# Input projection of a hybrid attention block: queries, SGU values and compressed keys/values with tokens stationary and weights moving

## The chip, the cores and the metric

The kernel runs on one core of a Trainium2 chip: TensorE (PE) with its weight loads (PEld), VectorE (DVE), ScalarE (ACT), GpSimd (POOL) and the DMA queues, one on SyncE (SP) and one on GpSimd. The metric is the device time of one execution in microseconds.

## The reference

One layer over 256 latent tokens with 256 context tokens as a prefix; everything is fp32, the model is 2048 wide. What matters here is the first half:

```python
h = _modulate(_rms(x, norm1_g), sh1, sc1)             # ctx_h likewise, from the context
proj = h @ w_in     # columns: q 512 | kv 256 + rotary key 64 | u 1024 | v 1024 | gates 4096
q = _rms(proj[:, :512], q_norm_g) @ w_uq              # 8 heads of 128 + 64, rotary, normed
kv = _rms(kv_in[:, :256], kv_norm_g) @ w_ukv          # kv_in: those columns of h and of ctx_h
k = _rms(concat([k_nope, k_rope]), qk_norm_k)
attn_o = attention(q, k, v)                           # over 512 keys
vn = layernorm(gelu(v_in)) * norm_g + norm_b
sgu_o = gelu(u_in) * (w_s @ vn + b_s)                 # in chunks of 128 tokens, 8 groups
merged = (sigmoid(ga) * (attn_o @ w_br_attn) + sigmoid(gb) * (sgu_o @ w_br_sgu)) @ w_out
```

After it stand a gated residual, a second norm and a SwiGLU feed-forward with 5632 hidden columns.

## The kernel before

**Precision.** A matrix product is made of three fp32r matmuls: both operands are split into a high part (`hi`, ACT copies to fp32r, line 230) and the difference (`lo`, DVE, line 231), and `mm3` adds hi x hi, hi x lo and lo x hi. Activations live in tiles `g` ("slots" of 128 x 512, 60 of them), with hi in columns 0 to 255 and lo in 256 to 511. `mm(out, lhsT, rhs)` (line 244) keeps `lhsT` in the array and streams `rhs`; in the profile `mm<-g,whi` is activations moving past standing weights, `mm<-whi,g` the other way round.

**Weights.** Class `W` loads them in pieces of 1024 columns (512 KB) into 10 buffers `raw` by SP's queue and splits each into parts of 512 columns in 8 buffers `whi` and 8 `wlo`.

**Input projection.** The string `ORDER` names the order of items: `M` (modulation vectors for some k-tiles of the hidden state, which end in the normed and split k-tiles `hs`, and `hc` for the context), `X` (loads the context), `C` (a chunk of the projection), `K` (a chunk of compressed keys/values), `A` (the norms of the latents). The 16 k-tiles come in six groups (`KGROUPS`: 2, 2, 2, 2, 4, 4), since they become ready one after the other; in each group all 24 column tiles of 128 are computed (`NT_IN`: 4 of Q, 8 of V, 8 of U, 4 of the gates) and added to the sums `acc` in SBUF, by ACT for the first group and by DVE (line 554) after. `in_chunk` and `kv_chunk` keep a weight tile of 128 x 128 standing and move 256 tokens, so the results have columns on partitions. `kv_chunk` has three column tiles, the third with the 64 rotary columns twice, for latents and context. PSUM has 4 banks `mm` for products and 4 `aux` for the rest. A scheduler orders the instructions of each engine; each engine then works in its order.

**Norms of the latents.** `latents` squares the sums, adds the squares over partitions and channels with fp32 matmuls against a matrix `ones`, makes 1/sqrt of whole rows of 256 or 512 columns (`rms_rstd`, `rsqrt`, lines 285 to 300), scales and splits.

**Gating (SGU).** V is needed with tokens on partitions for the layer norm, so PE transposes 16 tiles (line 650), ACT copies them out of PSUM (line 653), and DVE takes statistics. While this goes on, PE computes gate columns: `fill` hands out pieces of the rest of the gates (`fill_items`), and with each of them background pieces of the second modulation (`wmod2`), which DVE adds into `acc` (line 416) and whose results go through DRAM (`m_d`, lines 439 to 446, on POOL's queue).

**Attention.** Heads go in pairs. The factors `rk` of the key norms are written to DRAM (`rk_d`, line 757) and broadcast to 128 partitions, one DMA a head (line 782, POOL's queue), at the start of each pair; the first step of DVE on the scores (line 794) multiplies by them. ACT takes exp (line 800), DVE scales (line 802), PE transposes (line 805). `fill` again puts gate columns in between.

Of the kernel before, what the change touches and what calls it, by code (L numbers as in the profile page):

```python
# [13 lines left out]
P = 128  # L14
# [98 lines left out]
def block_kernel(  # L113
# [100 lines left out]
    class W:  # L214


        def __init__(self, src, ncols, split=True):
            self.raw = []
            self.parts = []
            for s in range(0, ncols, WHALF):  # L220
                n = min(WHALF, ncols - s)
                raw = wp.tile([P, WHALF], F32, tag="raw", name=f"raw{uid()}", bufs=RAW_BUFS)
                nc.sync.dma_start(raw[:, :n], src[P * s:P * (s + n)].rearrange("(p f) -> p f", p=P))
                self.raw.append(raw)
                if split:
                    for q in range(0, n, WPART):
                        e = min(WPART, n - q)
                        hi = wp.tile([P, WPART], F32R, tag="whi", name=f"whi{uid()}")
                        lo = wp.tile([P, WPART], F32R, tag="wlo", name=f"wlo{uid()}")
                        S.activation(hi[:, :e], raw[:, q:q + e], AF.Copy)  # L230
                        V.tensor_tensor(out=lo[:, :e], in0=raw[:, q:q + e], in1=hi[:, :e].bitcast(F32),  # L231
                                        op=ALU.subtract)
                        self.parts.append((hi, lo))

        def cols(self, c0, n=P):
            hi, lo = self.parts[c0 // WPART]
            c0 %= WPART
            return hi[:, c0:c0 + n], lo[:, c0:c0 + n]
# [239 lines left out]

    def latents(acc_q, acc_kv):
# [7 lines left out]
        rq0 = slot()  # L487
        rms_rstd(rq0[:, 0:256], ps[:, 0:256], Q_LORA, 256)
        for k in range(4):
            v = slot()[:, 0:256]  # L490
            V.scalar_tensor_tensor(out=v, in0=acc_q[k // 2][:, (k % 2) * 256:(k % 2 + 1) * 256],
                                   scalar=pcol(PR_QN + k), in1=rq0[:, 0:256], op0=ALU.mult, op1=ALU.mult)
            t = slot(F32R)
            split_to(t[:, 0:256], t[:, 256:512], v)
            qn.append(t)


        ps = auxbank()
        for k in range(2):
            sq = slot()  # L500
            S.activation(sq, acc_kv[k], AF.Square)
            mm(ps, ones, sq, k == 0, k == 1)
        rk0 = slot()
        rms_rstd(rk0, ps, KV_LORA, 512)
        for k in range(2):
            v = slot()
            V.scalar_tensor_tensor(out=v, in0=acc_kv[k], scalar=pcol(PR_KVN + k), in1=rk0,
                                   op0=ALU.mult, op1=ALU.mult)
            hi, lo = slot(F32R), slot(F32R)
            split_to(hi, lo, v)  # L510
# [10 lines left out]
    acc = [slot() for _ in range(NT_IN // 2)]  # L521
# [15 lines left out]
    def in_chunk(g, ts):  # L537
        ks = KGROUPS[g]
        nk = len(ks)
        n = len(ts) * nk * P  # L540
        w = W(flat(win, off[0], n), n)
        off[0] += P * n
        for ti, t in enumerate(ts):
# [4 lines left out]
            for ki, k in enumerate(ks):  # L548
                mm3(ps[:, h * 256:(h + 1) * 256], w.cols((ti * nk + ki) * P), hilo(hs[k]),
                    ki == 0, ki == nk - 1)  # L550
            if h == 1 and g == 0:
                S.activation(acc[i], ps, AF.Copy)
            elif h == 1:
                V.tensor_tensor(out=acc[i], in0=ps, in1=acc[i], op=ALU.add)  # L554

    acc_kv = [slot() for _ in range(NT_KV)]
    koff = [0]

    def kv_chunk(ks):
        nk = len(ks)  # L560
        w = W(flat(wkv, koff[0], NT_KV * nk * P), NT_KV * nk * P)
        koff[0] += P * NT_KV * nk * P
        for t in range(NT_KV):
            ps = mmbank()
            for src, o in ((hs, 0), (hc, 256)):
                for ki, k in enumerate(ks):
                    mm3(ps[:, o:o + 256], w.cols((t * nk + ki) * P), hilo(src[k]), ki == 0, ki == nk - 1)
            if ks[0] == 0:
# [8 lines left out]
            "A": [lambda: latents(acc[0:2], acc_kv)]}  # L577
# [59 lines left out]
    for i in range(4):  # L637
        S.activation(acc_v[i], acc_v[i], AF.Gelu)
# [119 lines left out]

    fill(UQ_GATES[4], GATE_RATE)
# [16 lines left out]
    for p in range(HEADS // 2):  # L776
        pair = (2 * p, 2 * p + 1)
        rkb, pts = {}, {}
        for h in pair:
            rkb[h] = slot()  # L780
            r = 2 * (h % 4) + h // 4
            nc.gpsimd.dma_start(rkb[h], rk_d[r:r + 1, :].to_broadcast([P, 512]))
# [228 lines left out]
def _layout(inp):  # L1011
# [44 lines left out]
    for ang in (row, col):  # L1056
# [79 lines left out]
```

## Time and profile before

| | |
|---|---|
| median of 3 runs | 1457.03 us (1454.49 to 1457.6) |
| profiled execution | 1455.91 us, its span 1454.1 us |
| PE busy | 1422.4 us (98% of the span), 8782 matmul records |
| DVE, ACT busy | 1018.6 us (70%), 772.6 us (53%) |
| DMA | 356.08 MB, mean 245 GB/s |
| granted TensorE clock, mean | 0.995 |

The span is the time from the first to the last instruction; the rest of the execution lies around it. "Busy" on PE counts the modelled length of matmuls, which overlap, so what one matmul costs is read from the distance between starts. The columns of a timeline are: start in us, length in us, engine, line, operation, out<-in, shape, count of merged instructions, and in brackets the idle time before and what ended it.

### The profile page before, as it was taken

Reading aid. Unit: us, or ns where it says so; the run is one execution under the profiler, and the core shown is the slowest. Engines: PE = TensorE matmul, PEld = TensorE weight load, DVE = VectorE, ACT = ScalarE, POOL = GpSimd, SP = SyncE. Lnnn points to the kernel's source line nnn. Section 1 sums busy time; section 2 is a strip of 40 time slices with the busy share of each in tenths; the row PEclk is TensorE's granted clock in tenths of the full one; section 3 lists DMA queues with packets and bytes.
Section 4 is the critical chain, followed back from the end, with each engine's and each line's share of the span. In section 5 each row is a group of like instructions: output and inputs, shape, how many; then the busy total and the mean of one; then the engine's idle time right before and its main releaser. Section 6 shows DMA issues by size and latency. Waiting matters only on the chain.

```text
span 1454.1 us, 23911 instructions
## 1 busy us (share of the span) xinstructions
PE 1422.4 (98%) x8782; PEld 1215.1 (84%) x8782; DVE 1018.6 (70%) x1738; ACT 772.6 (53%) x1432; POOL 22.2 (2%) x44
## 2 busy tenths in 40 slices
PE   6999999999989999999999999999999999999998
PEld 4898899886767799988788888888888888888887
DVE  2676579896688688999866666666666667786553
ACT  4655457555534554555566555555555554444442
POOL 0000000000101000000000000000000000000000
PEclk9999999999999999999999999999999999999999
DMA  9987874785499498999553555555555568898560
GB/s 366 350 318 266 316 297 140 253 287 190 144 313 314 175 362 329 324 353 391 175 183 135 192 188 186 192 188 189 187 190 189 188 202 308 309 361 302 198 213 33
DMA packets 104167, 356.08 MB, mean 245 GB/s; under 512 B 12520, under 2 KB 14824, under 8 KB 104048
## 3 DMA queue, kind: packets, MB, share of 16 engines
q1 hardware_dynamic: 102096, 350.82, 67.0%
q0 software_dynamic: 1952, 3.72, 1.0%
q8 instruction: 69, 1.13, 0.3%
q14 instruction: 50, 0.41, 0.1%
HBM read 352.36 MB, written 2.13 MB: 244 GB/s over the span
## 4 chain that ended last, share of the span: by engine, by line
PE 65%; DVE 4%; DMA 1%; issue 1%; ACT 0%; DVEq 0%; ACTq 0%
PE mm L244 62%; PE ax L244 2%; DVE acc L416 1%; DMA raw<-in_wmod_dram 1%; DVE wlo L231 1%; PE ax L805 0%; DVE g L802 0%; ACT g L800 0%; DVE g L405 0%; DVE g L890 0%; DVE g L794 0%; DVE g L870 0%; DVE g L892 0%; ACT whi L230 0%; DVE g L402 0%
## 5 line engine op out<-in xcount | busy, mean ns | idle before, releaser
L244 PE MATMUL mm<-g,whi 128*128 128x512 f32 (+1 forms) x3456 | 878.6, 347 | 0.8 <-ACT g L702 0.5
L230 ACT ACTIVATE whi<-raw 128x512 fp32r<-128x512 f32 x897 | 557.3, 630 | 500.9 <-PE mm L244 349.9
L231 DVE TENSOR_TENSOR wlo<-raw,whi 128x512 fp32r<-128x512 f32 x897 | 604.1, 687 | 259.1 <-ACT whi L230 253.4
L244 PE MATMUL mm<-g,wlo 128*128 128x256 f32 x2656 | 588.7, 282 | 0.6 <-DVE wlo L231 0.6
L244 PEld LDWEIGHTS mm<-g,wlo 128*128 128x128 f32 x2656 | 495.3, 190 | 79.5 <-DVE wlo L231 1.3
L244 PEld LDWEIGHTS mm<-g,whi 128*128 128x128 f32 x3456 | 540.0, 191 | 22.1 <-issue 11.0
L244 PE MATMUL mm<-whi,g 128*128 128x512 f32 x992 | 308.3, 391 | 0.0
L244 PEld LDWEIGHTS mm<-whi,g 128*128 128x128 f32 x992 | 186.2, 188 | 41.3 <-issue 2.5
L244 PE MATMUL mm<-wlo,g 128*128 128x512 f32 x496 | 193.2, 390 | 0.2 <-DVE wlo L231 0.2
L416 DVE SCALAR_TENSOR_TENSOR acc<-raw,silw,acc 128x1024 f32<-128x1024 f32 x120 | 153.4, 1278 | 17.7 <-DMA raw<-in_wmod_dram 17.1
L244 PEld LDWEIGHTS mm<-wlo,g 128*128 128x128 f32 x496 | 93.1, 188 | 21.2 <-issue 1.1
L554 DVE TENSOR_TENSOR g<-mm,g 128x512 f32<-128x512 f32 x60 | 41.1, 686 | 26.4 <-PE mm L244 25.9
L279 ACT ACTIVATE g<-g 128x256 fp32r<-128x256 f32 (+1 forms) x106 | 41.9, 414 | 13.7 <-DVE g L973 8.2
L280 DVE TENSOR_TENSOR g<-g,g 128x256 fp32r<-128x256 f32 (+1 forms) x106 | 43.2, 424 | 7.4 <-ACT g L279 7.3
L971 DVE TENSOR_TENSOR g<-mm,g 128x256 f32<-128x256 f32 x88 | 33.3, 419 | 17.3 <-ACT g L970 17.2
L970 ACT ACTIVATE g<-mm 128x256 f32<-128x256 f32 x88 | 29.0, 381 | 30.9 <-PE mm L244 30.9
L244 PE MATMUL ax<-g,g 128*128 128x128 f32 (+2 forms) x224 | 42.6, 374 | 0.0
L244 PE MATMUL ax<-raw,silw 128*32 128x256 f32 (+1 forms) x576 | 33.4, 359 | 3.7 <-DMA raw<-in_wmod_dram 3.7
L244 PEld LDWEIGHTS ax<-g,g 128*128 128x128 f32 (+1 forms) x224 | 26.6, 190 | 11.5 <-issue 9.6
L244 PEld LDWEIGHTS ax<-raw,silw 128*32 128x32 f32 x576 | 16.9, 109 | 16.0 <-DMA raw<-in_wmod_dram 5.8
L800 ACT ACTIVATE g<-g,nb,rq 128x512 f32<-128x512 f32 x16 | 13.0, 812 | 17.5 <-DVE nb L798 17.4
L375 ACT ACTIVATE g<-g,m 128x256 f32<-128x256 f32 x32 | 17.6, 592 | 8.3 <-DVE m L364 5.3
(140 smaller groups left out, 471.1 us busy)
## 6 DMA issues: line engine op xcount, KB each, us to landing
raw<-in_wmod_dram SPq DMA_DIRECT2D x192, 512.0 KB, 6.3
raw<-in_wffi_dram SPq DMA_DIRECT2D x176, 512.0 KB, 3.2
raw<-in_wffo_dram SPq DMA_DIRECT2D x88, 512.0 KB, 4.9
raw<-in_wgate_dram SPq DMA_DIRECT2D x56, 512.0 KB, 4.7
raw<-in_win_dram SPq DMA_DIRECT2D x48, 512.0 KB, 7.7
raw<-in_wout_dram SPq DMA_DIRECT2D x32, 512.0 KB, 7.5
raw<-in_wbrs_dram SPq DMA_DIRECT2D x16, 512.0 KB, 9.2
raw<-in_wbra_dram SPq DMA_DIRECT2D x16, 512.0 KB, 6.5
```

What stands on the lines that cost most here:

```text
L230: S.activation(hi[:, :e], raw[:, q:q + e], AF.Copy)
L231: V.tensor_tensor(out=lo[:, :e], in0=raw[:, q:q + e], in1=hi[:, :e].bitcast(F32), op=ALU.subtract)
L244: nc.tensor.matmul(out, lhsT, rhs, start=start, stop=stop)
L279: S.activation(dst_hi, src, AF.Copy)
L280: V.tensor_tensor(out=dst_lo, in0=src, in1=dst_hi.bitcast(F32), op=ALU.subtract)
L375: S.activation(v, v, AF.Identity, bias=m[:, 2 * jj + s:2 * jj + s + 1], scale=m[:, 2 * n + 2 * jj + s:2 * n + 1 + 2 * jj + s])
L416: V.scalar_tensor_tensor(out=acc, in0=w.raw[0], scalar=sil[:, k, 0:1], in1=acc, op0=ALU.mult, op1=ALU.add)
L554: V.tensor_tensor(out=acc[i], in0=ps, in1=acc[i], op=ALU.add)
L800: exp = S.activation(t, t, AF.Exp, bias=nb, scale=rq[:, col:col + 1], accum_out=sm)
L970: S.activation(d, ps[:, 256:512], AF.Copy)
L971: V.tensor_tensor(out=d, in0=ps[:, 0:256], in1=d, op=ALU.add)
```

## The change

Q, V and the compressed keys/values are computed the other way round: 128 tokens stand (`rows_of`: the hi or lo half of a k-tile of `hs`), and 512 (Q: one block, V: two, called `T`) or 320 weight columns move. The results have tokens on partitions: a `T` block fills two banks, one for each half of the tokens; kv makes four tiles of 128 tokens x 320. U and the gates stay (`F`). Weight pieces of kv are 960 columns, its parts 320. The latents' norms are taken by rows (`unit_rows`: an ACT square with its sum, small operations on 128 x 2 or 128 x 4, a DVE scaling), and PE then transposes the normed rows (8 tiles for Q, 12 for kv), after which `scaled_parts` applies the gain and splits. V needs no transposes in the gating stage. The broadcasts of `rk` are issued one head pair ahead (`key_rows`), odd pairs into `rst` and a part of `cst` that are no longer read.

```diff
+    items = [("T", b) for b in range(NB_T)] + [("F", t) for t in range(NT_F)]
...
+    def unit_rows(tiles, n):
+
+        ssq = small(len(tiles), f"ssq{n}", 1)
+        for i, t in enumerate(tiles):
+            S.activation(slot()[:, 0:n], t[:, 0:n], AF.Square, accum_out=ssq[:, i:i + 1])
+        r = small(len(tiles), f"rr{n}", 1)
+        rms_rstd(r, ssq, n, len(tiles))
+        for i, t in enumerate(tiles):
+            V.tensor_scalar_mul(t[:, 0:n], t[:, 0:n], r[:, i:i + 1])
...
+        unit_rows(acc_q, Q_LORA)
         for i in range(2):
-            sq = slot()
-            S.activation(sq, acc_q[i], AF.Square)
-            for k in range(2):
-                mm(ps[:, 0:256], ones, sq[:, k * 256:(k + 1) * 256], i + k == 0, i + k == 2)
...
+            ps = auxbank()
+            for j in range(2):
+                for tt in range(2):
+                    k = 2 * i + j
+                    nc.tensor.transpose(ps[:, j * 256 + tt * P:j * 256 + (tt + 1) * P],
+                                        acc_q[tt][:, k * P:(k + 1) * P], ident)
...
+            if kind == "T":
+                ps = [mmbank(), mmbank()]
+                for ki, k in enumerate(ks):
+                    for tt in range(2):
+                        mm3(ps[tt], rows_of(hs, k, tt), w.cols(c0 + ki * 512, 512), ki == 0, ki == nk - 1)
+                for tt in range(2):
+                    summed(g, acc_t[t][tt], ps[tt])
...
-        for t in range(NT_KV):
-            ps = mmbank()
-            for src, o in ((hs, 0), (hc, 256)):
-                for ki, k in enumerate(ks):
-                    mm3(ps[:, o:o + 256], w.cols((t * nk + ki) * P), hilo(src[k]), ki == 0, ki == nk - 1)
...
+        for t, src in enumerate((hs, hs, hc, hc)):
+            ps = mmbank()[:, 0:KV_COLS]
+            for ki, k in enumerate(ks):
+                mm3(ps, rows_of(src, k, t % 2), w.cols(ki * KV_COLS, KV_COLS), ki == 0, ki == nk - 1)
+            summed(ks[0], acc_kv[t][:, 0:KV_COLS], ps)
...
-            ps = auxbank()
-            for i in range(4):
-                j = half * 4 + i
-                nc.tensor.transpose(ps[:, i * P:(i + 1) * P],
-                                    acc_v[j // 2][:, (j % 2) * 256 + n * P:(j % 2) * 256 + (n + 1) * P], ident)
-            d = slot()
-            S.activation(d, ps, AF.Copy)
-            V.bn_stats(out=st[:, half * 6:(half + 1) * 6], in_=d)
-            nat.append(d)
+            V.bn_stats(out=st[:, half * 6:(half + 1) * 6], in_=nat[half])
...
+        for h in (2 * p, 2 * p + 1):
+            rkb[h] = slot() if p % 2 == 0 else (rst, cst[:, 2 * P:2 * P + TOK])[h % 2]
...
+        if p + 1 < HEADS // 2:
+            key_rows(p + 1)
```

On PE, the first chunk of the projection before the change; the product banks are `mm`, the first name behind the arrow moves, the second stands (`g_230` and `g_287` are the first two k-tiles):

```order
L244 MATMUL mm_310<-g_230,whi_292 128x256 x2
L244 MATMUL mm_310<-g_230,wlo_293 128x256
L244 MATMUL mm_324<-g_230,whi_296 128x256 x2
L244 MATMUL mm_310<-g_287,whi_292 128x256
L244 MATMUL mm_324<-g_230,wlo_297 128x256
L244 MATMUL mm_324<-g_287,whi_296 128x256
```

The same place after it (`g_231` and `g_288` are the k-tiles now; line 244 has become 255):

```order
L255 MATMUL mm_311<-whi_293,g_231 128x512
L255 MATMUL mm_312<-whi_293,g_231 128x512
L255 MATMUL mm_311<-wlo_294,g_231 128x512
L255 MATMUL mm_311<-whi_293,g_231 128x512
L255 MATMUL mm_312<-wlo_294,g_231 128x512
L255 MATMUL mm_312<-whi_293,g_231 128x512
L255 MATMUL mm_311<-whi_297,g_288 128x512
```

Weights and tokens have changed sides, a matmul is 512 columns wide, and two banks are filled together.

On PE at the norm of Q's latents before the change, in the last third of the chunk after Q's last one (`ax_2798` is the bank of the sums):

```order
L244 MATMUL mm_2772<-g_2403,whi_2742 128x256 x2
L244 MATMUL mm_2772<-g_2403,wlo_2743 128x256
L244 MATMUL ax_2798<-g_2799,ones 128x256 x2
L244 MATMUL ax_2798<-g_2803,ones 128x256 x2
L244 MATMUL mm_2896<-g_2102,whi_2878 128x256 x2
L244 MATMUL mm_2896<-g_2102,wlo_2879 128x256
```

After it, between the first V block (`mm_2429`, `mm_2430`; called T1 below, Q's block is T0) and the second (`mm_2576`, T2); `g_161` and `g_162` are the normed rows of Q:

```order
L255 MATMUL mm_2430<-wlo_2426,g_2128 128x512
L255 MATMUL mm_2430<-whi_2425,g_2128 128x512
L512 MATMUL ax_2474<-cst,g_161 128x128
L512 MATMUL ax_2474<-cst,g_162 128x128
L512 MATMUL ax_2474<-cst,g_161 128x128
L512 MATMUL ax_2474<-cst,g_162 128x128
L512 MATMUL ax_2485<-cst,g_161 128x128
L512 MATMUL ax_2485<-cst,g_162 128x128
L512 MATMUL ax_2485<-cst,g_161 128x128
L512 MATMUL ax_2485<-cst,g_162 128x128
L255 MATMUL mm_2576<-whi_2558,g_1875 128x512
```

On DVE, what makes those rows ready stands like this after the change (line 561 adds T0's two banks, 242 is the split of weights, 310 to 305 the small operations, 498 the scaling):

```order
L561 TENSOR_TENSOR g_161<-mm_2381,g_161 128x512
L561 TENSOR_TENSOR g_162<-mm_2382,g_162 128x512
L242 TENSOR_TENSOR wlo_2573<-raw_2566,whi_2572 128x512
L310 TENSOR_SCALAR g_2463<-ssq_2457 128x2
L242 TENSOR_TENSOR wlo_2607<-raw_2604,whi_2606 128x512
L302 RECIPROCAL g_2465<-g_2465 128x2
L303 TENSOR_TENSOR g_2466<-g_2463,g_2465 128x2
L242 TENSOR_TENSOR wlo_2611<-raw_2604,whi_2610 128x512
L304 SCALAR_TENSOR_TENSOR g_2466<-g_2466,g_2465 128x2
L305 SCALAR_TENSOR_TENSOR rr_2462<-g_2466,g_2465 128x2
L498 TENSOR_SCALAR g_161<-g_161,rr_2462 128x512
L498 TENSOR_SCALAR g_162<-g_162,rr_2462 128x512
```

The transposes depend on the end of this chain, where the `ones` matmuls depended on the squares alone. The 12 transposes of kv stand 24 + 33 matmuls further on.

On POOL, the DMA issues around the head pairs before the change:

```order
L757 DMA rk_d<-g_4439 2x512 x4
L782 DMA g_4546<-rk_d 128x512
L782 DMA g_4548<-rk_d 128x512
L439 DMA m_d_4823<-g_4821 16x1x16 x4
L442 DMA sh_158<-m_d_4823 128x8x1
L782 DMA g_4922<-rk_d 128x512
L782 DMA g_4924<-rk_d 128x512
```

And after it:

```order
L783 DMA rk_d<-g_4067 2x512 x4
L793 DMA g_4082<-rk_d 128x512
L793 DMA g_4084<-rk_d 128x512
L793 DMA rst<-rk_d 128x512
L793 DMA cst<-rk_d 128x512
L450 DMA m_d_4453<-g_4451 16x1x16 x4
L453 DMA sh_158<-m_d_4453 128x8x1
L793 DMA g_4552<-rk_d 128x512
L793 DMA g_4554<-rk_d 128x512
```

The second pair's broadcasts (`rst`, `cst`) stand ahead of the `m_d` transfers now, right behind the first pair's.

## Rows read from the trace of the kernel before

**Rows 1.** Busy time on the page: us, share of the span, instructions.

```profile
PE 1422.4 (98%) x8782; PEld 1215.1 (84%) x8782; DVE 1018.6 (70%) x1738; ACT 772.6 (53%) x1432; POOL 22.2 (2%) x44
```

**Rows 2.** Stretches: length, busy us by engine, granted PE clock, DMA share, GB/s.

```profile
24.00:212.00 188.00, 184.82 (x1719) 166.50 (x1720) 124.25 (x238) 97.15 (x192) 0.00 (x0) 0.98 0.83 320
212.00:300.00 88.00, 87.97 (x600) 80.76 (x599) 77.45 (x143) 57.57 (x99) 0.00 (x0) 1.00 0.61 210
...
397.00:480.00 83.00, 76.27 (x420) 59.37 (x420) 72.48 (x120) 35.56 (x70) 9.43 (x16) 0.96 0.90 309
```

**Rows 3.** Timeline of PE in the input projection; eight triples lie between the two.

```profile
70.81 0.28 PE L244 MATMUL mm<-g,wlo 128*128 128x256 f32 x1
...
73.69 0.28 PE L244 MATMUL mm<-g,wlo 128*128 128x256 f32 x1
```

**Rows 4.** Timeline of PE in the last projection; eight triples lie between the two.

```profile
1222.14 0.39 PE L244 MATMUL mm<-wlo,g 128*128 128x512 f32 x1
...
1227.58 0.39 PE L244 MATMUL mm<-wlo,g 128*128 128x512 f32 x1
```

**Rows 5.** Timeline of PE at Q's norm and at the gating stage's transposes.

```profile
216.60 0.28 PE L244 MATMUL mm<-g,wlo 128*128 128x256 f32 x1
216.72 1.89 PE L244 MATMUL ax<-g,ones 128*128 128x256 f32 x8
...
218.68 0.28 PE L244 MATMUL mm<-g,wlo 128*128 128x256 f32 x1
...
266.00 1.91 PE L650 MATMUL ax<-cst,g 128*128 128x128 f32 x16
```

**Rows 6.** Timeline at the second norm, whose chain is the nearest to the new one.

```profile
705.98 0.63 ACT L893 ACTIVATE g<-g 128x512 f32<-128x512 f32 x1 [3.06 <-DVE g L892]
706.52 0.19 ACT L893 ACTIVATION_READ_ACCUMULATOR g<-g 128x1 f32 x1
...
708.19 0.38 PE L244 MATMUL ax<-dg,g 128*128 128x128 f32 x1 [1.65 <-DVE dg L908]
```

**Rows 7.** Groups by line and shape: busy us, mean ns, idle us before, its releasers.

```profile
L231 DVE TENSOR_TENSOR wlo<-raw,whi 128x512 fp32r<-128x512 f32 x895 | 603.5, 688 | 259.1 <-ACT whi L230 253.4 <-DMA raw<-in_wffi_dram 2.8 <-DMA raw<-in_wmod_dram 0.3
...
L230 ACT ACTIVATE whi<-raw 128x512 fp32r<-128x512 f32 x895 | 556.7, 630 | 500.9 <-PE mm L244 349.9 <-DVE wlo L231 70.1 <-DMA raw<-in_win_dram 26.8
...
L554 DVE TENSOR_TENSOR g<-mm,g 128x512 f32<-128x512 f32 x60 | 41.1, 686 | 26.4 <-PE mm L244 25.9
...
L802 DVE TENSOR_SCALAR g<-g,sm 128x512 f32<-128x512 f32 x16 | 7.7, 483 | 0.3
...
L290 ACT ACT_TABLE_LOAD x4 | 5.1, 1283 | 0.1
```

**Rows 8.** Timelines of POOL, DVE and PE at the second head pair.

```profile
404.53 1.09 POOL L782 DMA_DIRECT2D g<-rk_d  x2
...
412.52 0.69 DVE L794 CUSTOM_DVE_ANT_0 g<-ax,g 128x512 f32<-128x512 f32 x1 [3.29 <-DMA g<-rk_d]
...
412.91 0.40 PE L244 MATMUL mm<-g,whi 128*128 128x512 f32 x1
416.97 0.45 PE L805 MATMUL ax<-cst,g 128*128 128x128 f32 x1 [3.66 <-DVE g L802]
```

**Rows 9.** Two stretches behind that gap, columns as in rows 2.

```profile
416.90:422.50 5.60, 5.53 (x19) 4.89 (x20) 5.02 (x9) 2.12 (x5) 0.00 (x0) 0.50 0.83 251
422.60:428.00 5.40, 5.40 (x31) 4.43 (x31) 4.70 (x7) 2.71 (x5) 0.00 (x0) 1.00 0.97 351
```

**Rows 10.** The third pair: issue, landing of these broadcasts, DVE's step, PE's wait.

```profile
446.76 0.56 POOL L782 DMA_DIRECT2D g<-rk_d  x1
...
DMA to landing us min/median/max: 6.5/7.5/8.6
...
453.44 0.69 DVE L794 CUSTOM_DVE_ANT_0 g<-ax,g 128x512 f32<-128x512 f32 x1 [2.37 <-PE mm L244]
...
458.41 0.63 PE L805 MATMUL ax<-cst,g 128*128 128x128 f32 x4 [2.49 <-DVE g L802]
```

More of the change, by code (lines that the diff above doesn't have):

```diff
@@ L99, in in_chunks @@
 def in_chunks():
+    items = [("T", b) for b in range(NB_T)] + [("F", t) for t in range(NT_F)]
     out = []
     for g, ks in enumerate(KGROUPS):
-        c = max(1, (WCOLS // P) // len(ks))
-        out += [(g, list(range(i, min(i + c, NT_IN)))) for i in range(0, NT_IN, c)]
+        room = 0
+        for it in items:
+            if room == 0:
+                out.append((g, []))
+                room = WCOLS // P // len(ks)
+            out[-1][1].append(it)
+            room -= 4 if it[0] == "T" else 1
     return out
@@ new lines, in latents @@
+            for j in range(2):
+                t = slot(F32R)
+                scaled_parts(t[:, 0:256], t[:, 256:512], ps[:, j * 256:(j + 1) * 256], pcol(PR_QN + 2 * i + j))
+                qn.append(t)
+        unit_rows(acc_kv, KV_LORA)
+        for t in acc_kv:
+            V.tensor_copy(t[:, KV_COLS:KV_COLS + ROPE], t[:, KV_LORA:KV_COLS])
+        turned_kv = []
+        for k in range(3):
+            ps = auxbank()
+            for tt in range(4):
+                nc.tensor.transpose(ps[:, tt * P:(tt + 1) * P], acc_kv[tt][:, k * P:(k + 1) * P], ident)
+            turned_kv.append(ps)
@@ L518, in latents @@
         V.tensor_copy(krot[:, 256:512], kg[:, 256:512])
-    acc = [slot() for _ in range(NT_IN // 2)]
+    acc_t = [[slot() for _ in range(2)] for _ in range(NB_T)]
+    acc = [slot() for _ in range(NT_F // 2)]
     chunks = in_chunks()
@@ L535, in block_kernel, with summed, rows_of, in_chunk @@
     pcur = {}
-    def in_chunk(g, ts):
+    def summed(g, d, ps):
+        if g == 0:
+            S.activation(d, ps, AF.Copy)
+        else:
+            V.tensor_tensor(out=d, in0=ps, in1=d, op=ALU.add)
+    def rows_of(src, k, tt):
+        return src[k][:, tt * P:(tt + 1) * P], src[k][:, 256 + tt * P:256 + (tt + 1) * P]
+    def in_chunk(g, items):
         ks = KGROUPS[g]
         nk = len(ks)
-        n = len(ts) * nk * P
+        n = sum(4 if kind == "T" else 1 for kind, _ in items) * nk * P
         w = W(flat(win, off[0], n), n)
         off[0] += P * n
-        for ti, t in enumerate(ts):
+        c0 = 0
+        for kind, t in items:
+            if kind == "T":
[5 more added lines that the diff above has]
+                    summed(g, acc_t[t][tt], ps[tt])
+                c0 += nk * 512
+                continue
             i, h = divmod(t, 2)
@@ L548, in in_chunk @@
             for ki, k in enumerate(ks):
[L549 to L556, printed above, removed]
+                mm3(ps[:, h * 256:(h + 1) * 256], w.cols(c0 + ki * P), hilo(hs[k]), ki == 0, ki == nk - 1)
+            if h == 1:
+                summed(g, acc[i], ps)
+            c0 += nk * P
+    acc_kv = [slot() for _ in range(4)]
     koff = [0]
@@ L576, in block_kernel @@
             "K": [lambda ks=ks: kv_chunk(ks) for ks in kv_groups()],
-            "A": [lambda: latents(acc[0:2], acc_kv)]}
+            "A": [lambda: latents(acc_t[0], acc_kv)]}
     for o in ORDER:
         todo[o].pop(0)()
-    acc_v = [acc[2 + i] for i in range(4)]
-    acc_u = [acc[6 + i] for i in range(4)]
-    gate_a, gate_b = acc[(NT_IN - NT_GE) // 2:], []
+    acc_v = acc_t[NB_Q:]
+    acc_u = acc[0:NT_U // 2]
+    gate_a, gate_b = acc[NT_U // 2:], []
     sgo = []
@@ L636, in block_kernel @@
     sg = [row_bcast(RW_SG + i) for i in range(4)]
-    for i in range(4):
-        S.activation(acc_v[i], acc_v[i], AF.Gelu)
+    for v in acc_v:
+        for t in v:
+            S.activation(t, t, AF.Gelu)
     for i in range(4):
@@ L777, in block_kernel @@
         pair = (2 * p, 2 * p + 1)
[L778 to L782, printed above, removed]
+        pts = {}
+        if p + 1 < HEADS // 2:
+            key_rows(p + 1)
         for qt in range(2):
```

84 lines of the change are left out of this document (36 added, 48 removed).

## Prediction

> **What bounds the kernel now.** I read the totals first. TensorE (PE) is busy 1422.4 of 1454.1 us [rows 1], so the question is where it waits and where it is only kept full. The table by stretches answers that: in the input projection (24 to 212 us) it is busy 184.8 of 188 us, while the DMA engines are busy 83% of the time; in the gating stretch (212 to 300) it is busy 87.97 of 88; in the attention (397 to 480) it is busy 76.3 of 83, with VectorE (DVE) at 72.5 and the DMA engines at 90%, and the granted clock averages 0.96 [rows 2]. So up to 300 us work taken from PE is time, as long as ScalarE (ACT) and DVE deliver; in the attention waits count.
>
> **Price of a matmul.** In the input projection eight triples of 256 columns, from 70.81 to 73.69 us, take 2.88 us, which is 120 ns a matmul [rows 3]. In the last projection, where weights move and tokens stand, eight triples of 512 columns take 5.44 us, 226.7 ns each [rows 4]. At 2.4 GHz (the granted clock averages 0.98 over the first stretch [rows 2]) 256 columns alone are 106.7 ns and 512 are 213.3, so both rows leave 13.3 ns for each matmul with its own weight load. Fewer, wider matmuls save 13.3 ns each.
>
> **Token blocks (T).** Twelve column tiles, Q's 4 and V's 8, were 12 x 16 x 3 = 576 matmuls of 256 columns; they become 3 x 16 x 2 x 3 = 288 of 512, the same columns. 576 x 120 - 288 x 226.7 ns = 69.1 - 65.3: **-3.8 us**.
>
> The page "TensorE: Matmul & The Clock Gate" of the Trainium skill, section "Back-to-back issue gap", gives an isolated matmul its columns at 2.4 GHz plus about 2.5 ns. By that this term would be -0.7 us, and the kv term below -5.4. The trace disagrees, with 13.3 ns at both widths.
>
> **Compressed keys/values (kv).** Before: 3 tiles, the third the rotary columns twice, x 2 sources x 16 x 3 = 288 matmuls of 256. After: 4 token tiles x 16 x 3 = 192 of 320, the rotary columns once. No row has 320 columns. The bounds are the two rows, 120 and 226.7 ns: 192 of them take 23.0 to 43.5 us against 34.6 before, so from -11.5 to +9.0. I take the straight line between them, 146.7 ns, because both rows lie on it with the same 13.3 ns: 28.2 us, **-6.4 us**.
>
> **Norms of the latents.** Removed on PE: the matmuls against `ones`. Between the matmul at 216.60 and that at 218.68 us 0.36 us would pass without them; 2.08 did, so Q's four cost 1.7 us [rows 5]; kv's two have twice the columns each, so I estimate as much again. Added: 8 and 12 transposes. Sixteen such ran in the gating stage in 1.91 us, end of the last included [rows 5]; started one behind the other that is some 0.11 us each, 2.2 us for 20. Together **-1.2 us**. The 16 of the gating stage, where PE has no gap [rows 2], go: **-1.8 us**; the four ACT copies behind them cost nothing, since PE had work of the gates over them.
>
> **The wait that this adds.** Before, PE needed only squares for its `ones` matmuls, and the long row arithmetic ran beside other matmuls. Now PE's transposes need the whole chain: add, square, root, scale. The nearest chain of its kind (line 893 to the transposing matmuls of the second norm) takes 2.21 us from the square's start, with PE waiting the last 1.65 of them [rows 6]. Q's stands in the order behind one block, T1, of 24 matmuls: 5.4 us of cover. From the end of T0 I count the second add 0.69, one weight copy 0.63, two squares of about 0.8 with their accumulators, a weight copy 0.63, then the small operations, about 1.4 (706.71 to 708.19 in rows 6), two weight differences of 0.69 among them, and two scalings of 0.48 [rows 6, 7]: 6.4 us with what overlaps. So PE waits some 1.0 us. Behind the transposes stands T2, and everything after it. The kv transposes have T2 and 33 matmuls of 256 as cover, 9.4 us, and ahead of them in ACT's queue lie Q's four scaled copies, a Gelu, some four weight copies, four squares and two table loads of 1.28 [rows 7], about 10 us, and then DVE's chain of about 3: 2 us late. **+3 us**; bounds 0 (the scheduler placed them to fit) and 7 (both chains twice as late).
>
> **Banks and weight parts.** A block holds two PSUM banks and fills them together, so the third block waits for both adds of the first; a kv group holds all its weight parts until its fourth token tile, where before they came free one by one. Each add is 0.69 us, and DVE had time over before them: of 60 adds the queue stood idle before many, 25.9 us in all, waiting for PE [rows 7]. The DMA engines at 83% have room too; if PE needs 10 us less of 188 the share is about 88%. I take **+1.5 us**, bounds 0 and 5.
>
> **Key rows (rk) ahead.** Before, the second head pair's two broadcasts were issued at 404.53 us, and the score step of DVE (line 794) sat idle 3.29 us until 412.52 for the first of them; PE had run out at 413.3 and stood until 416.97, 3.66 us [rows 8]. Behind that gap the clock is at half: 19 matmuls in 5.6 us, and 31 in the 5.4 us after it at full clock [rows 9], so 2.3 us more are lost. The third pair's step began at 453.44, after 2.37 us of idleness that the view puts on PE; these broadcasts land 6.5 to 8.6 us after issue, and were issued from 446.76 on, so I read it as the broadcast again; PE then waited 2.49 us [rows 10]. Now each pair's broadcasts stand in GpSimd's queue one pair (some 35 us) earlier, ahead of the `m_d` stores, which wait for ACT anyway. PE's upper bound is 3.66 + 2.3 + 2.49 = 8.5 us. But DVE has only 10.5 us of idleness in those 83 us, 5.7 of it this wait, and the DMA engines 8 [rows 2, 8, 10]: what is late next is DVE's own queue and the weights. I take **-5 us**, bounds 0 and -8.5.
>
> **Sum.** -3.8 - 6.4 - 1.2 - 1.8 + 3 + 1.5 - 5 = -13.7. The profiled execution took 1455.9 us (span 1454.1 and 1.8 around it), so 1442.2; it lies 1.1 under the median of the runs, so by the median 1457.0 - 13.7 = **1443 us**.
>
> **Rivals.**
> - *The broadcasts are hidden, but another wait takes their place*: PE's gaps at 413 and 456 stay, with half a clock behind the first. For it: DVE and DMA are nearly full there. Against: DVE stood idle in both gaps. 1448 us.
> - *The chains of the norms eat the gain*: both waits and the banks at their upper bounds, +12 instead of +4.5: 1451 us. For it: ACT's queue in order. Against: before, PE waited nowhere in that stretch.
> - *320 columns cost what 512 do*: +9.0 instead of -6.4, 1458 us, no change. Only the missing row speaks for it.
> - *Slower: a stop of PE at the transposes long enough to drop the clock*, as after the 3.66 us gap. It decides when the two stops add up to more than 15 us (instead of 3), each with 2.3 us at half clock behind it; two stops of 9 us give 1463. Against it: the whole Q chain counted above is 6.4 us and has 5.4 of cover.
> - *The 13.3 ns belong to the columns, not to the matmul*: then T gives nothing, and kv gives its columns alone, 61,440 for 73,728, a sixth of 34.6, 5.8 us. Against it: the two rows have the same rest at 256 and at 512 columns [rows 3, 4]. 1448 us. The Trainium skill's section cited above comes near this case with its 2.5 ns a matmul; the trace speaks against both.
>
> **How the numbers follow.** Forecast (1437 to 1447, its own range) 0.62; other wait in the attention 0.13; chains 0.10; columns 0.04; slower 0.03; smaller gap 0.03; below 1437, all hidden and the attention giving 8.5, 0.05. From 1436 to 1450 I hold 0.8. A change within 0.2% (2.9 us) can't be told from none: faster 0.91 (all but the chains' far end, columns and slower), same 0.05, slower 0.04.
>
> **What would show it.** Right: in the input projection 512-column matmuls with weights moving 227 ns apart and the 320 ones 147; the gating stretch starts some 7 us earlier; a wait of about 1 us before the Q transposes and 2 before kv's; no idle DVE before the second pair's scores; no half clock in the attention. Wrong: gaps of more than 3 us at the transposes, gaps before the third block of a group, or the attention as long as before.

## The result and the profile after

The changed kernel takes **1431.7 us** (median of 4 runs, 1430.63 to 1432.35) against 1457.3 (the kernel before, now with four runs), a ratio of 0.9828 [0.9811, 0.9845]: 25.6 us faster. The forecast was 1443, with 1437 to 1447 as its own range and a chance of 0.8 for 1436 to 1450, so the sign was right and the size was wrong. The profiled execution took 1432.35 us with a span of 1430.5.

The page's first block, after [rows 1]:

```profile
span 1430.5 us, 23109 instructions
PE 1403.3 (98%) x8390; PEld 1187.3 (83%) x8390; DVE 1009.4 (71%) x1748; ACT 766.0 (54%) x1438; POOL 21.9 (2%) x44
```

PE was busy 19.1 us less (in which is what half clock had added, 2.3 by [rows 9]); the rest of the 23.6 us of span is waiting that went. I cut both traces at the same instructions and compared the lengths. The cuts are the first matmul of the projection, the last against `silw` (the modulation), the first of the gates that moves 512 columns, the first against `unit` (the key norms), DVE's first and last score step, and the first against `dg` (the second norm):

| stretch, us | before | after | difference | forecast |
|---|---|---|---|---|
| start to the projection | 23.81 | 24.25 | +0.44 | these three: |
| projection to the last `silw` matmul | 159.97 | 150.67 | -9.30 | -6.9 |
| to the first gate | 59.46 | 56.25 | -3.21 | |
| gating, to the key norms | 94.98 | 92.30 | -2.68 | -1.8 |
| key norms to the first score | 36.82 | 33.16 | -3.66 | these two: |
| first to last score | 125.47 | 120.36 | -5.11 | -5 |
| all behind | 953.58 | 953.51 | -0.07 | 0 |

The gate pieces that fill PE moved between the two attention stretches, so only their sum, -8.77, is to be read.

The same views as rows 2, after. Columns: length; busy us (instructions) of PE, PEld, DVE, ACT, POOL; granted clock; DMA share; GB/s:

```profile
24.00:203.00 179.00, 175.44 (x1389) 147.28 (x1390) 124.00 (x248) 96.59 (x202) 0.00 (x0) 0.99 0.87 333
203.00:291.00 88.00, 87.64 (x567) 79.08 (x566) 75.65 (x153) 53.93 (x101) 0.00 (x0) 1.00 0.65 232
380.00:463.00 83.00, 80.62 (x466) 62.55 (x464) 75.77 (x127) 39.15 (x79) 8.09 (x14) 1.00 0.92 336
```

The last row answers to 397 to 480 before, the same place in the work: PE busy 80.6 instead of 76.3 us, DVE 75.8 instead of 72.5, and no half clock. In the first the DMA share is 0.87, where I had said 88%.

**The new shapes.** Timeline of PE: a token block, and a kv tile:

```profile
73.20 0.62 PE L255 MATMUL mm<-whi,g 128*128 128x512 f32 x2
...
79.32 0.62 PE L255 MATMUL mm<-whi,g 128*128 128x512 f32 x2
...
187.46 0.31 PE L255 MATMUL mm<-wlo,g 128*128 128x320 f32 x1
...
194.06 0.31 PE L255 MATMUL mm<-wlo,g 128*128 128x320 f32 x1
```

Nine triples of 512 columns take 6.12 us, 226.7 ns each [rows 4]; fifteen triples of 320 columns take 6.60, 146.7 ns each, to the digit the value that was interpolated.

**The transposes.** Timeline of DVE at Q's chain, and of PE at Q's and kv's transposes:

```profile
199.93 1.28 DVE L561 TENSOR_TENSOR g<-mm,g 128x512 f32<-128x512 f32 x2
...
202.01 0.17 DVE L310 TENSOR_SCALAR g<-ssq 128x2 f32<-128x2 f32 x1 [0.21 <-ACT g L494]
...
204.25 0.16 DVE L305 SCALAR_TENSOR_TENSOR rr<-g,g 128x2 f32<-128x2 f32 x1
204.45 0.88 DVE L498 TENSOR_SCALAR g<-g,rr 128x512 f32<-128x512 f32 x2
```

```profile
205.03 0.40 PE L255 MATMUL mm<-whi,g 128*128 128x512 f32 x1
205.26 1.11 PE L512 MATMUL ax<-cst,g 128*128 128x128 f32 x8
206.13 0.47 PE L255 MATMUL mm<-whi,g 128*128 128x512 f32 x1
...
215.53 0.28 PE L255 MATMUL mm<-g,wlo 128*128 128x256 f32 x1
215.94 1.66 PE L527 MATMUL ax<-cst,g 128*128 128x128 f32 x12
```

The chain runs from 199.93 to 205.33, 5.4 us; T1 is as long, and its last matmul issued at 205.03, 0.23 us ahead of the transposes: no wait. Ahead of kv's transposes PE lost some 0.3 us (0.41 between starts, of which a matmul is 0.12). Q's eight transposes took 0.87 us, as priced.

**The scores of the second and third pair.** DVE and PE [rows 8, 10]:

```profile
392.25 0.69 DVE L829 CUSTOM_DVE_ANT_0 g<-ax,rst 128x512 f32<-128x512 f32 x1
...
396.70 0.63 PE L840 MATMUL ax<-cst,g 128*128 128x128 f32 x4 [0.56 <-DVE g L837]
...
441.17 0.63 PE L840 MATMUL ax<-cst,g 128*128 128x128 f32 x4 [1.20 <-DVE g L837]
```

And the issues of the broadcasts into `rst` (number; ns each; first and last start, us):

```profile
L793 POOL DMA_DIRECT2D rst<-rk_d x2: 537/546/556, 353.5 to 409.0; - x2
```

The second pair's was issued at 353.5, 38.7 us ahead of the step that reads it, and DVE does not wait for it; PE's waits of 3.66 and 2.49 us have become 0.56 and 1.20, and the four transposes take 0.63 us instead of the 1.09 that they take at half clock. All of PE's waits for scaled scores between the first and last score step (us in total, times, longest), before, after, and in e2 below, which is the kernel before with early broadcasts:

```profile
PE ax L805 <- DVE g L802: 9.6, 10, 3.7
```

```profile
PE ax L840 <- DVE g L837: 4.8, 10, 1.2
```

```profile
PE ax L812 <- DVE g L809: 3.9, 10, 0.8
```

### The profile page after: what moved, and what is told of

Read it like the earlier page. It is cut to its first block, busy times and chain, and to the rows that moved or that the text cites. A ratio compares the mean times of both kernels' runs of the same rounds, so it can differ in the third digit from the quotient of the medians.

```text
span 1430.5 us, 23109 instructions
## 1 busy us (share of the span) xinstructions
PE 1403.3 (98%) x8390; PEld 1187.3 (83%) x8390; DVE 1009.4 (71%) x1748; ACT 766.0 (54%) x1438; POOL 21.9 (2%) x44
## 4 chain that ended last, share of the span: by engine, by line
PE 86%; DVE 6%; DMA 5%; issue 2%; ACT 2%; SPq 0%; POOL 0%; DVEq 0%; ACTq 0%; POOLq 0%
PE mm L255 80%; PE ax L255 5%; DVE wlo L242 2%; DVE acc L427 2%; DMA raw<-in_wmod_dram 1%; DMA raw<-in_win_dram 1%; DMA raw<-in_wout_dram 1%; PE ax L840 1%; DMA g<-in_rows_dram 0%; ACT whi L241 0%; DMA m_d<-g 0%; DMA sh<-m_d 0%; DVE g L837 0%; ACT g L386 0%; DMA g<-in_xT_dram 0%
## 5 line engine op out<-in xcount | busy, mean ns | idle before, releaser
L241 ACT ACTIVATE whi<-raw 128x512 fp32r<-128x512 f32 (+1 forms) x900 | 555.4, 627 | 481.8 <-PE mm L255 334.8
L242 DVE TENSOR_TENSOR wlo<-raw,whi 128x512 fp32r<-128x512 f32 (+1 forms) x900 | 603.8, 685 | 263.5 <-ACT whi L241 255.1
L255 PE MATMUL mm<-g,whi 128*128 128x512 f32 (+1 forms) x2880 | 767.9, 357 | 0.0
L255 PE MATMUL mm<-g,wlo 128*128 128x256 f32 x2368 | 505.3, 281 | 0.0
L255 PEld LDWEIGHTS mm<-g,wlo 128*128 128x128 f32 x2368 | 438.3, 189 | 78.9 <-issue 2.0
L255 PEld LDWEIGHTS mm<-g,whi 128*128 128x128 f32 x2880 | 447.9, 190 | 14.6 <-issue 8.3
L255 PE MATMUL mm<-whi,g 128*128 128x512 f32 (+1 forms) x1312 | 401.3, 385 | 1.9 <-ACT whi L241 1.2
L255 PEld LDWEIGHTS mm<-whi,g 128*128 128x128 f32 x1312 | 244.6, 189 | 53.9 <-issue 3.7
L255 PE MATMUL mm<-wlo,g 128*128 128x512 f32 (+1 forms) x656 | 251.5, 384 | 0.7 <-DVE wlo L242 0.7
L561 DVE TENSOR_TENSOR g<-mm,g 128x512 f32<-128x512 f32 (+1 forms) x72 | 46.3, 654 | 23.4 <-PE mm L255 22.9
L386 ACT ACTIVATE g<-g,m 128x256 f32<-128x256 f32 x32 | 17.6, 593 | 10.2 <-DVE m L375 5.8
```

The source lines that it names most:

```text
L255: nc.tensor.matmul(out, lhsT, rhs, start=start, stop=stop)
L386: S.activation(v, v, AF.Identity, bias=m[:, 2 * jj + s:2 * jj + s + 1], scale=m[:, 2 * n + 2 * jj + s:2 * n + 1 + 2 * jj + s])
L561: V.tensor_tensor(out=d, in0=ps, in1=d, op=ALU.add)
```

## The experiments

The theory after the result: the prices of matmuls were right; the waits that I added to the sum hardly came (0.3 us at the transposes), since the transposes stand where their chain is done; and the early broadcasts gave as much as their upper bound. The rival: waits came as forecast, and the blocks or kv gave more than 13.3 ns a matmul can explain. "Changed kernel" is the kernel after the change, 1431.7 us. The median of the kernel before was 1457.15 us beside e1 to e4, 1455.74 beside e6, e7, e9 and e10, and 1456.92 beside e5, e8, e11 and e12, so between groups the ratios are compared.

**Broadcasts late again, in the changed kernel (e1), and early, in the kernel before (e2).** The edit of e1; e2 is its reverse, in the old kernel:

```
-            rkb[h] = slot() if p % 2 == 0 else (rst, cst[:, 2 * P:2 * P + TOK])[h % 2]
+            rkb[h] = slot()
...
-    key_rows(0)
...
-        if p + 1 < HEADS // 2:
-            key_rows(p + 1)
+        key_rows(p)
```

> The changed kernel with the broadcasts of rk at the start of their own pair again, in slots. Theory (the broadcasts alone made the attention's gaps, and these the half clock): the 8.8 us that the stretch from the key norms to the last score step lost come back, 1440.5 us, with a PE gap of 3 us or more before a pair's first transposes and a stretch at half clock behind it. Rival (the attention gained because the pieces before it arrive in another order): within 1 us of the changed kernel, 1431.7.

> The kernel before with only the broadcasts of rk one pair ahead. Theory: the attention gains the same 8.8 us without the rest of the change, 1457.3 - 8.8 = 1448.5 us, and the half clock at 416 us is gone. Rival (DVE and the weights are late next, as the prediction had it): -5 us or less, 1452 to 1457.

Measured: e1 1440.1 us (1437.55 to 1441.56), ratio 0.9885 [0.987, 0.99], 8.4 us slower than the changed kernel; e2 1448.63 (1448.29 to 1449.37), ratio 0.9946 [0.9931, 0.9961], 8.5 us faster than the kernel before. Both ways the move is worth as much as the upper bound. DVE and PE in e1, then the two stretches around its stop:

```profile
395.92 0.69 DVE L827 CUSTOM_DVE_ANT_0 g<-ax,g 128x512 f32<-128x512 f32 x1 [2.65 <-DMA g<-rk_d]
...
400.37 1.09 PE L838 MATMUL ax<-cst,g 128*128 128x128 f32 x4 [3.04 <-DVE g L835]
...
434.83 0.69 DVE L827 CUSTOM_DVE_ANT_0 g<-ax,g 128x512 f32<-128x512 f32 x1 [1.68 <-DMA g<-rk_d]
...
439.81 0.63 PE L838 MATMUL ax<-cst,g 128*128 128x128 f32 x4 [1.80 <-DVE g L835]
```

```profile
400.40:404.00 3.60, 3.60 (x16) 3.21 (x17) 3.13 (x7) 1.40 (x3) 0.00 (x0) 0.62 0.77 300
404.00:408.50 4.50, 4.50 (x29) 3.94 (x28) 4.40 (x7) 2.75 (x6) 0.00 (x0) 1.00 0.85 283
```

The gaps of rows 8 and 10 are back, at both pairs and with the same releaser, and a stretch at half clock behind the first. At the third pair the view now names the broadcast, as rows 10 had been read. This profile is of the shortest of e1's four runs, 5.3 us of span above the changed kernel. The others have no trace, but their mean granted clocks are 0.996, 0.994 and 0.994 against 0.997 here; 0.003 of 1438 us is, as an estimate, 4.3 us more lost to half clock in the last two, which took 4.0 and 2.8 us longer. By this estimate what the trace doesn't show is mostly half clock. In e2, over the 83 us of rows 2:

```profile
397.00:480.00 83.00, 81.50 (x466) 62.71 (x465) 75.80 (x128) 38.92 (x78) 8.12 (x14) 1.00 0.92 336
```

PE is busy 81.5 of 83 us, with the DMA engines at 92% and DVE at 75.8 us: neither had been full before.

**A token block's matmul as two of 256 columns (e3); kv with the rotary columns twice, 384 wide (e4).** What they undo (e4 also loads kv's weights in pieces of two parts instead of three and leaves out four small copies of the rotary columns):

```
-                        mm3(ps[tt], rows_of(hs, k, tt), w.cols(c0 + ki * 512, 512), ki == 0, ki == nk - 1)
+                            mm3(ps[tt][:, h:h + 256], rows_of(hs, k, tt), w.cols(c0 + ki * 512 + h, 256), ...
```

```
-KV_COLS = KV_LORA + ROPE
+KV_COLS = KV_LORA + 2 * ROPE
```

> The changed kernel with each T matmul of 512 columns made as two of 256, tokens still standing, columns and adds the same: 288 more matmuls. Theory (13.3 ns a matmul): +3.8 us, 1435.5. Rivals: the isolated gap of the page, 2.5 ns a matmul, +0.7, 1432.4; and if the gain of the projection came from the order of the work rather than from fewer matmuls, no change either.

> The changed kernel with kv's matmuls 384 columns wide (the rotary columns twice in the weights, so that no small copies are needed). Theory (columns at 2.4 GHz plus 13.3 ns): 173.3 ns each, 192 x 26.7 ns = +5.1 us, 1436.8. Rival (a width that is not 256 or 512 costs what 512 does): no change, 1431.7. The DMA of a fifth more kv weights should be hidden.

Measured: e3 1434.86 us (1433.14 to 1435.1), ratio 0.9848 [0.9831, 0.9864], 3.2 more; e4 1436.52 (1435.46 to 1437.46), ratio 0.9862 [0.9847, 0.9877], 4.8 more. PE in e3, then in e4:

```profile
73.60 0.28 PE L255 MATMUL mm<-wlo,g 128*128 128x256 f32 x1
...
78.64 0.28 PE L255 MATMUL mm<-wlo,g 128*128 128x256 f32 x1
```

```profile
190.47 0.34 PE L255 MATMUL mm<-wlo,g 128*128 128x384 f32 x1
...
198.27 0.33 PE L255 MATMUL mm<-wlo,g 128*128 128x384 f32 x1
```

In e3 fourteen triples in 5.04 us are 120.0 ns a matmul, with the weights moving, as before the change with the tokens moving. In e4 fifteen triples in 7.80 us are 173.3 ns: 160 of columns at 2.4 GHz and 13.3 again. So 13.3 ns stand beside the columns at 256, 320, 384 and 512, and the rival on the blocks' and kv's worth falls. The spacing is the firmer evidence, since e3's 3.2 us is not the 288 matmuls alone: its profiled run also stood at half clock where the changed kernel's did not:

```profile
39.20:42.60 3.40, 3.40 (x18) 3.40 (x18) 2.06 (x4) 2.41 (x6) 0.00 (x0) 0.50 1.03 410
```

The page "TensorE: Matmul & The Clock Gate" of the Trainium skill, section "Back-to-back issue gap", puts 2.5 ns there for an isolated matmul, by which e3 would have cost an estimated 0.7 us; these matmuls, each with a weight load of its own, disagree.

**The chains behind the transposes: squares done twice (e6), the same with T2 held behind Q's transposes (e9), no cover at all (e10).**

```
+            S.activation(slot()[:, 0:n], t[:, 0:n], AF.Square)
             S.activation(slot()[:, 0:n], t[:, 0:n], AF.Square, accum_out=ssq[:, i:i + 1])
```

e9 and e10 let the matmuls of the blocks that are written behind the latents' step issue after Q's transposes; e10 has the squares once and that step one chunk earlier (`CCACCCC` to `CACCCCC`):

```
+                with ExitStack() as held:
+                    for i in turned_q:
+                        held.enter_context(tc.issue_after(i.ins))
```

> The changed kernel (1431.7 us) with each square of the latents' rows done twice, the first into a scratch tile, so that the two chains behind Q's and kv's transposes get longer: two more squares of 0.63 us on ScalarE for Q (1.3 us), four of 256 columns for kv (some 1.6 us); the output is the same. Theory, that the wait never came because the scheduler places the transposes behind as much other work as the chain needs: in this kernel's order Q's eight transposes stand 13 matmuls of 512 columns later, inside block T2, and kv's later too, so TensorE waits under 0.3 us at either place and the time is 1431.7 to 1432.5 us. Rival, that the chain is in line with the product as the prediction counted it, so that what is added to it is added to the time: 1.3 + 1.6 us more, 1434.6 us.

> As the run with the squares done twice, but with block T2 held behind Q's transposes on TensorE, so that T1's 24 matmuls (5.4 us) are all the cover that Q's chain has, as the prediction assumed. Theory: the chain is 5.4 us in the changed kernel (first sum of T0 to the end of the second scaling), so with 1.3 us more TensorE stands 1.0 to 1.5 us ahead of these eight transposes, and the time is 1433.0 us, 1.3 more than the run without the hold. Rival, that the chain has slack even so: no wait, 1431.7 us. A third reading, the prediction's own count of 6.4 us: a wait of 2.3 us, 1434.0 us.

> The changed kernel with the latents' step written one chunk earlier and blocks T1 and T2 held behind Q's transposes, so that Q's chain has no cover on TensorE at all; the squares are done once. Theory: TensorE stands for the whole chain, 5.4 us, at one place; if a stop of that length also drops the granted clock as the 3.66 us gap of the kernel before did, some 2.3 us more are lost behind it: 1437.1 to 1439.4 us. Rival, the prediction's slower case (two stops of 9 us): not reached by Q's chain alone, since 9 us would give 1440.7 and with the clock 1443.0 us. If the chain overlaps with work that TensorE still has, 1433 to 1435 us.

Measured: e6 1430.83 us (1430.61 to 1431.53), ratio 0.9828 [0.9813, 0.9843], that of the changed kernel; e9 1435.62 (1433.08 to 1436.38), 0.9857 [0.9842, 0.9872]; e10 1437.3 (1436.56 to 1438.8), 0.9873 [0.9857, 0.989]. PE at Q's transposes in e6, in e9 and in e10:

```profile
208.06 0.62 PE L255 MATMUL mm<-whi,g 128*128 128x512 f32 x2
208.51 1.20 PE L513 MATMUL ax<-cst,g 128*128 128x128 f32 x8
```

```profile
205.04 0.39 PE L255 MATMUL mm<-whi,g 128*128 128x512 f32 x1
208.14 1.97 PE L513 MATMUL ax<-cst,g 128*128 128x128 f32 x8 [2.72 <-DVE g L499]
```

```profile
198.94 0.39 PE L255 MATMUL mm<-whi,g 128*128 128x512 f32 x1
203.14 2.15 PE L512 MATMUL ax<-cst,g 128*128 128x128 f32 x8 [3.80 <-DVE g L498]
```

In e6 the scheduler put the transposes 13 matmuls further on, and a chain that is longer by two squares costs nothing: the place of the transposes follows the chain. With that freedom taken away in e9, PE stops for 2.72 us; from the last `silw` matmul to the first gate 4.0 us are added to the changed kernel's, so 1.3 more went behind the stop, where the clock is at half:

```profile
208.10:210.00 1.90, 1.86 (x9) 1.75 (x10) 1.58 (x3) 0.98 (x2) 0.00 (x0) 0.50 0.71 259
```

It stops longer than the two squares (1.3 us), and DVE's rows say why:

```profile
203.07 0.17 DVE L310 TENSOR_SCALAR g<-ssq 128x2 f32<-128x2 f32 x1 [1.25 <-ACT g L495]
...
204.86 1.29 DVE L562 TENSOR_TENSOR g<-mm,g 128x512 f32<-128x512 f32 x2
206.07 0.15 DVE L303 TENSOR_TENSOR g<-g,g 128x2 f32<-128x2 f32 x1
...
207.60 0.88 DVE L499 TENSOR_SCALAR g<-g,rr 128x512 f32<-128x512 f32 x2
```

Between the small operations stand T1's sums and weight differences, as in e6, where the transposes come later anyway; on the same queue the chain now takes 4.5 us from the first small operation to the first scaling, against 2.4 in the changed kernel. In e10 nothing covers the chain; PE stops for 3.80 us, and that stretch of the span is 6.4 longer, 2.6 of it behind the stop, at half clock:

```profile
203.10:205.00 1.90, 1.86 (x9) 1.65 (x9) 0.40 (x2) 0.47 (x1) 0.00 (x0) 0.50 0.34 138
205.00:207.00 2.00, 2.00 (x7) 1.61 (x6) 1.33 (x3) 0.93 (x3) 0.00 (x0) 0.50 0.00 0
207.00:209.00 2.00, 2.00 (x6) 1.54 (x6) 0.48 (x1) 2.00 (x10) 0.00 (x0) 0.60 0.00 0
```

So the slower rival's mechanism exists, and even without any cover Q's chain would have cost 6.4 us, not the 15 from which that rival decides. kv's chain was not tried without cover.

**More work at the sums: a copy of each bank ahead of the sum (e7), a copy of the summed tile behind it (e11).**

```
+                    V.tensor_copy(slot(), ps[tt])
                     summed(g, acc_t[t][tt], ps[tt])
```

> The changed kernel with each sum of a token block's bank preceded by a copy of that bank to scratch on VectorE: the bank is held some 0.7 us longer and VectorE has 30 more operations (some 21 us) in the input projection; the output is the same. Theory, that banks and sums have room there (the term of 1.5 us for banks and weight parts did not come): under 1 us more, 1431.7 to 1432.7 us. Rival, that banks are tight since two fill together, so that the third block waits for both adds of the first: at least 0.7 us at each of some 15 blocks, 10 us, 1441 us.

> The changed kernel with the same extra VectorE work as the run with copies ahead of the sums, but behind them: a copy of the summed tile to scratch, so that the bank is free as early as in the changed kernel and only VectorE's queue is longer. That run was 3.5 us slower than the changed kernel (1435.2). Theory A, that there it was the bank held longer: now no loss, 1431.7 to 1432.5 us. Theory B, that it is VectorE's time, whose queue delays the weight differences: as slow as that run, 1434.5 to 1436 us.

Measured: e7 1435.2 us (1434.01 to 1436.62), 0.9857 [0.9843, 0.9872]; e11 1433.58 (1433.41 to 1435.51), 0.9841 [0.9826, 0.9856]. The stretches up to about where the changed kernel's first one ends, in e7 and in e11:

```profile
24.00:207.00 183.00, 178.37 (x1388) 147.07 (x1389) 141.60 (x282) 97.13 (x197) 0.00 (x0) 0.99 0.86 325
```

```profile
24.00:206.00 182.00, 177.89 (x1389) 147.12 (x1390) 134.83 (x282) 96.97 (x196) 0.00 (x0) 0.99 0.87 327
```

DVE does 17.6 and 10.8 us more there, and by the ratios 4 and 2 us are lost (the 2 lies within the intervals): neither nothing nor the 10 of tight banks. PE's waits for VectorE's sums come to 0.9 us in e7 and 0.2 in e11, so a bank held longer is a part of e7's loss. The copies behind the sums turned out cheaper than those from the bank, so for the rest these two don't part a bank held longer from a longer queue; that stays open. That the change itself lost little at the banks, PE's waits in the changed kernel show directly, from 24 to 203 us (releaser; us in total, times, longest):

```profile
PE ax L359 <- ACT g L356: 1.9, 3, 0.7
PE mm L255 <- ACT whi L241: 1.2, 1, 1.2
PE mm L255 <- ACT g L559: 0.6, 1, 0.6
PE mm L255 <- DVE wlo L242: 0.6, 1, 0.6
```

No wait is for one of VectorE's sums (line 561). One of 0.6 us, at 111.34, is for a bank all the same: kv's four tiles of the first group held the four `mm` banks until ScalarE had copied the first of them out (line 559), and a block waited for it. Before the change no wait for a bank stands in this stretch.

**The SGU values alone back in columns (e5).** The eight V tiles become "F" tiles again, with their sixteen transposes and ScalarE copies in the gating stretch:

```
-NB_Q, NB_V = 1, 2
+NB_Q, NT_V = 1, 8
...
-NT_F = NT_U + NT_GE
+NT_F = NT_V + NT_U + NT_GE
```

> The changed kernel with only the SGU values back in the old form: eight column tiles with weights standing, and their sixteen transposes and four copies on ScalarE in the gating stretch; Q's block, kv and the early broadcasts stay. Theory, that the terms for blocks and transposes are priced rightly and nothing else hangs on V: 192 matmuls more at 13.3 ns are 2.6 us, sixteen transposes 1.8 us, together 4.4: 1436.1 us. Rivals: without V's blocks Q's transposes have other work as cover and banks are freer, so it costs less, 1433.5 us; or the copies on ScalarE are no longer covered and it costs more, 1438.5 us.

Measured: 1439.57 us (1439.06 to 1440.66), 0.9881 [0.9865, 0.9898], 7.9 more instead of 4.4. PE's waits from 225 to 335 us say where the rest is:

```profile
PE mm L255 <- ACT g L735: 2.1, 1, 2.1
PE ax L255 <- DVE g L709: 1.7, 1, 1.7
```

The changed kernel has 0.2 us there, and the kernel before waited 0.5 us in all from 225 to 345 us. So in this mixture 3.6 of the 7.9 us are waits, which I put down to the SGU's longer chain without cover; that is argued and not tried. The 4.3 us that are left are close to the 4.4 of the priced work.

**Gate pieces 2 and 2 instead of 0 and 4 at the third pair (e8), and 1 and 3 (e12).**

```
-ATT_GATES = [2, 2, 2, 2, 0, 4, 0, 2]
+ATT_GATES = [2, 2, 2, 2, 2, 2, 0, 2]
```

> The changed kernel with the gate pieces that fill the attention spread evenly over the third head pair (2 and 2 instead of 0 and 4). In the changed kernel TensorE still waits 1.2 us for VectorE's scaled probabilities at the third pair, and some 4.8 us in all such waits between the first and the last score step. Theory, that this one wait is for want of other work at that place: it goes, 1430.5 us. Rival, that it is VectorE's own queue: unchanged or moved, 1431.7 us. Slower, 1433 us, if the later half is left without fill.

> As the run with fills 2 and 2, but 1 and 3 at the third pair. Theory: part of that 1.2 us wait goes, 1431.0 us; rival: unchanged, 1431.7 us.

Measured: e8 1431.52 us (1431.13 to 1433.38), 0.9826 [0.9812, 0.9841]; e12 1431.18 (1430.89 to 1431.48), 0.9822 [0.9807, 0.9836]. In both PE's wait of 1.20 us at the third pair is gone (the longest left is 0.7); e12, from 320 to 480 us:

```profile
PE ax L840 <- DVE g L837: 3.6, 9, 0.7
```

It was 4.8 us in 10 waits. A gain of that size can't be told from none here, so no version is shown to beat the changed kernel.

## Why the prediction was wrong in size

- *Token blocks -3.8, kv -6.4*: right. The rows give 226.7 and 146.7 ns; undone in part, e3 cost 3.2 and e4 4.8 (5.1 by the rows).
- *Norms of the latents -1.2*: not tried alone. The first three stretches of the table together gave -12.1; blocks, kv and norms as priced are -11.4. The other 0.7 us I don't split.
- *SGU transposes -1.8*: the stretch gave -2.7. Of the other 0.9 us, 0.3 are in PE's waits (0.5 before, 0.2 after); the rest I don't split.
- *The wait that this adds +3*: failed; 0.3 us came. For Q I counted 6.4 us of chain against 5.4 of cover, and the chain is 5.4. Up to the first small operation it took 2.1 us (199.93 to 202.01), where I had put 3.6 of add, weight copies and squares behind one another before taking off an overlap: the copies ran beside the adds and the first small operation. For kv I wrote 2 us, though my own 10 and 3 us against 9.4 of cover give 3.6. From Q's first scaled copy at 206.06 us, ScalarE's part took 8.2 us instead of 10, and DVE's up to the first scaled tile 1.7 instead of 3: 9.8 in all. I had also taken the order as given, and it isn't given either: e6 moved the transposes behind a longer chain at no cost, and in e9, where this is forbidden, PE stops. Bound 0 ("the scheduler placed them to fit") was nearly right.
- *Banks and weight parts +1.5*: the mechanism failed. No block waited for VectorE's adds and no weight part was missed at kv; the one wait for a bank, 0.6 us, was for kv's tiles and ScalarE. PE's waits for weight parts are 1.8 us against 0.9 before, of which 1.2 lie ahead of the very first block. That these add up to near 1.5 would be luck, and the stretches, which gave more than the priced terms, don't show it as a loss.
- *Key rows ahead -5*: the mechanism was right, the size wrong: -8.8 in the profile, 8.4 and 8.5 in e1 and e2, where the upper bound was 8.5. The step that failed is "what is late next is DVE's own queue and the weights". DVE's 10.5 us of idleness were more than the 8.5 to be gained, and the DMA engines went from 90% to 92% without PE waiting for them. That the bound was met so closely is in part luck: of the two gaps, 6.15 us, 1.8 stay in the changed kernel and 0.9 in e2, and smaller waits shrank too. PE's waits at the scores (9.6 to 4.8 us) and 2.3 of half clock make 7.1 of the 8.8 us, in e2 (9.6 to 3.9) 8.0 of the 8.5; the rest is in no wait that I saw.

With these two added terms at 0 and the broadcasts at 8.5 the same sum gives -21.7, 1435 by the median; the stretches gave -23.6, and the 1.9 between is in the 0.7, 0.9 and 0.3 named above. The profiled execution of before lay 1.4 us under 1457.3 and that of after 0.7 over 1431.7, which is the way from 23.6 to 25.6. The forecast's own "all hidden and the attention giving 8.5" was the case that came, with a chance of 0.05, and even that case lay 3.6 us above the measured time.

## What to carry to other kernels

Where a scheduler orders the instructions, as here, a dependent instruction stands where the scheduler expects its input to be ready: before a wait is added to a sum, ask whether the order would move if the chain were longer. For a gap with a named releaser, work out "nearly full" before a discount is taken for it: the idle time of the engine that is said to be late next, against the time to be gained. Here there was more idle time than gain, and the move gave as much as the gaps and their half clock. And what a stop costs isn't only the stop: look at the granted clock behind it.

## What the runs showed of the hardware

A matmul with its own weight load took its columns at 2.4 GHz and 13.3 ns: 120.0 ns at 256 columns, with tokens moving [rows 3] and with weights moving (e3), and 146.7, 173.3 and 226.7 ns at 320, 384 and 512.

Stops of PE in full work of 2.72 (e9), 3.04 (e1), 3.80 (e10) and 3.66 us [rows 8] were each followed by a stretch at half clock; that of 2.49 us [rows 10] was not. Stops alone don't tell it all: in e3 the clock stood at half from 39.2 us on, behind a run of 64 matmuls of the modulation and two waits of 0.7 us. Half clock cost 1.3 us behind the stop of 2.72 and 2.6 behind that of 3.80, so in e9 a wait of under 3 us cost half as much again.
